# Row kurtosis on one core: load shapes, mixed sums, a halved last square, per-partition scaling and a warm TensorE

## The chip, the cores and the metric

The kernel runs on one core of one Trainium2 chip. The metric is device time in microseconds (us) of one execution, median over runs. All runs told here are of the state "fast". PE is TensorE, DVE is VectorE, ACT is ScalarE, POOL is GpSimd, SP is the engine that issues the loads. PSUM is the memory that this kernel has PE write its sums to (the pools `psum` and `psfin`).

## The reference

```python
# x: 1024 x 8192, float32
mean = np.mean(x, axis=-1, keepdims=True)
std = np.std(x, axis=-1, keepdims=True)
z = (x - mean) / (std + 1e-8)
return (np.mean(z ** 4, axis=-1) - 3).astype(np.float32)
```

With d = x - mean, the result per row is N sum(d^4) / (sum(d^2))^2 - 3. Every element is read once (33.5 MB), squared once after the mean is known, and squared again.

## The kernel before

The rows are worked in 18 groups; the results of several groups, a batch (`BATCHES`), are finished together and leave in one output transfer. A group of `k = 2` holds 64 rows, each split over two partitions, so a tile is 128 x 4096 float32 (2 MB). Group by group: PE transposes the tile in 128-column pieces and adds them up in PSUM, DVE adds partition pairs (`red`), a product gives the negated mean, ACT squares with the mean as bias and writes the sum of squares, then ACT does the first 512 columns of the fourth powers and DVE the other 3584.

```python
GROUPS = [(8, [1024], 0), (8, [1024], 0), (4, [2048], 0),
    (2, [2048, 2048], 512),            # ... ten of these, groups 3 to 12
    (2, [1536, 1536, 1024], 512),      # ... four, groups 13 to 16
    (2, [1536, 1280, 768, 512], 2816)] # group 17: k, pieces of the load, ACT's columns
BATCHES = [[0, 1], [2], [3, ..., 14], [15, 16, 17]]   # (cut)
# ...
small = ctx.enter_context(tc.tile_pool(name="small", bufs=4))
fin = ctx.enter_context(tc.tile_pool(name="fin", bufs=3))
# ... in finish(b), once for each batch:
kr = fin.tile([n, r], f32, name="kr")
nc.vector.tensor_mul(kr, p4, rec2)
nc.vector.tensor_scalar_add(kr, kr, -3.0)
dst = out[ROWS[b[0]]:ROWS[b[-1] + 1]].rearrange("(g r) -> g r", r=r)
nc.sync.dma_start(out=dst, in_=kr)
# ... the main part starts with all loads, on the same queue:
for i in range(NG):
    load(i)
```

Two things in these lines matter later. The pool `fin` gives each named tile `bufs` buffers in turn: with 2, the third `kr` takes the buffer of the first and waits until the transfer that reads the first is done (1.39 us of idle time in the changed kernel's trace, 3.71 in that of a_half); with 3 the fourth takes it, and in the traces of before and a_fin3 that one did not have to wait. And the four output transfers are issued by SP in program order, behind all the loads.

Of the kernel before, what the change touches and what calls it, by code (L numbers as in the profile page):

```python
# [7 lines left out]
f32 = mybir.dt.float32  # L8
bf16 = mybir.dt.bfloat16
AO = mybir.AluOpType  # L10
AF = mybir.ActivationFunctionType
P = 128
# [4 lines left out]
    (8, [1024], 0),  # L17
    (8, [1024], 0),
    (4, [2048], 0),
    (2, [2048, 2048], 512),  # L20
    (2, [2048, 2048], 512),
    (2, [2048, 2048], 512),
    (2, [2048, 2048], 512),
    (2, [2048, 2048], 512),
    (2, [2048, 2048], 512),
    (2, [2048, 2048], 512),
    (2, [2048, 2048], 512),
# [1 line left out]
    (2, [2048, 2048], 512),  # L29
    (2, [1536, 1536, 1024], 512),  # L30
    (2, [1536, 1536, 1024], 512),
    (2, [1536, 1536, 1024], 512),
    (2, [1536, 1536, 1024], 512),
    (2, [1536, 1280, 768, 512], 2816),
]
BATCHES = [[0, 1], [2], [3, 4, 5, 6, 7, 8, 9, 10, 11, 12, 13, 14], [15, 16, 17]]
SLOT_W = 4096
SLOTS = 12


@with_exitstack
def kernel(
    ctx: ExitStack,
    tc: tile.TileContext,
    x: bass.AP,
    out: bass.AP,
):
    nc = tc.nc
    n_rows, n_cols = x.shape
    neg_inv_n = -1.0 / float(n_cols)  # L50
    AX = mybir.AxisListType.X
    NG = len(GROUPS)
    L = NG - 1
    KS = [g[0] for g in GROUPS]
    ROWS = [sum(P // k for k in KS[:i]) for i in range(NG + 1)]
    assert ROWS[-1] == n_rows

    xpool = ctx.enter_context(tc.tile_pool(name="xpool", bufs=SLOTS))
    const = ctx.enter_context(tc.tile_pool(name="const", bufs=1))
    small = ctx.enter_context(tc.tile_pool(name="small", bufs=4))  # L60
    fin = ctx.enter_context(tc.tile_pool(name="fin", bufs=3))
    psum = ctx.enter_context(tc.tile_pool(name="psum", bufs=2, space=bass.MemoryType.PSUM))
    psfin = ctx.enter_context(tc.tile_pool(name="psfin", bufs=1, space=bass.MemoryType.PSUM))
    ctx.enter_context(tc.manual_schedule())

    warm = const.tile([P, 1], f32, name="warm")
    nc.vector.memset(warm, 0.0)
    nc.scalar.activation(out=warm, in_=warm, func=AF.Square)  # L68


    blk = {}

    def block_matrix(k):
        r = P // k
        b = const.tile([P, P], f32, name=f"blk{k}")
        v = b.rearrange("p (r k) -> p r k", k=k)
        nc.gpsimd.memset(b, neg_inv_n)
        nc.gpsimd.affine_select(  # L78
            out=v, in_=v, pattern=[[-k, r], [0, k]], base=0,
            channel_multiplier=1, compare_op=AO.is_ge, fill=0.0)  # L80
        nc.gpsimd.affine_select(  # L81
            out=v, in_=v, pattern=[[k, r], [0, k]], base=k - 1,
            channel_multiplier=-1, compare_op=AO.is_ge, fill=0.0)
        blk[k] = b

    for k in dict.fromkeys(k for k in KS if k > 2):
        block_matrix(k)
    ident = const.tile([P, P], f32, name="ident")
    nc.gpsimd.memset(ident, 1.0)
    nc.gpsimd.affine_select(  # L90
        out=ident, in_=ident, pattern=[[-1, P]], base=0,
        channel_multiplier=1, compare_op=AO.is_equal, fill=0.0)
    negcol = const.tile([P, 1], f32, name="negcol")
    nc.gpsimd.memset(negcol, neg_inv_n)
    block_matrix(2)
    junk = const.tile([P, 1024], bf16, name="junk")

    where = {}
    for b in BATCHES:
        n = len(b)  # L100
        sa = const.tile([P, 2 * n], f32, name=f"sa{b[0]}")
        sd = const.tile([P, n], f32, name=f"sd{b[0]}")
        nc.gpsimd.memset(sa, 0.0)
        for j, i in enumerate(b):
            where[i] = (j, n, sa, sd)

    xts = {}
    sums = {}
    nmus = {}

    def load(i):
        k, pieces, _ = GROUPS[i]
        w = n_cols // k
        assert sum(pieces) == w
        xt = xpool.tile([P, SLOT_W], f32, name="xt")
        xts[i] = xt[:, :w]
        src = x[ROWS[i]:ROWS[i + 1], :].rearrange("r (k w) -> (r k) w", k=k)
        c = 0
        for w in pieces:
            nc.sync.dma_start(out=xt[:, c:c + w], in_=src[:, c:c + w])  # L120
            c += w



    def row_sums(i):
        k = KS[i]
        xt = xts[i]
        w = n_cols // k
        if k == 2:
            tps = psum.tile([P, P], f32, name="tps")  # L130
            for c in range(0, w, P):
                nc.tensor.matmul(tps, lhsT=xt[:, c:c + P], rhs=ident,  # L132
                                 start=c == 0, stop=c == w - P, is_transpose=True)
            red = small.tile([P, P], f32, name="red")
            nc.vector.tensor_reduce(  # L135
                out=red.rearrange("p (r k) -> p r k", k=k),
                in_=tps.rearrange("p (r k) -> p r k", k=k).unsqueeze(2).to_broadcast(
                    [P, P // k, k, k]),
                op=AO.add, axis=AX)
            sums[i] = (red, negcol)  # L140
        else:
            part = small.tile([P, 1], f32, name="part")
            nc.vector.tensor_tensor_reduce(  # L143
                out=junk[:, :w // 2], in0=xt[:, :w // 2], in1=xt[:, w // 2:], scale=1.0, scalar=0.0,
                op0=AO.add, op1=AO.add, accum_out=part)
            sums[i] = (blk[k], part)

    def mean(i):
        mps = psum.tile([P, 1], f32, name="mps")
        lhs, rhs = sums[i]  # L150
        nc.tensor.matmul(mps, lhsT=lhs, rhs=rhs, start=True, stop=True)  # L151
        nmu = small.tile([P, 1], f32, name="nmu")
        nc.scalar.copy(nmu, mps)  # L153
        nmus[i] = nmu

    def square(i):
        j, n, sa, sd = where[i]
        nc.scalar.activation(out=xts[i], in_=xts[i], func=AF.Square, bias=nmus[i],  # L158
                             accum_out=sa[:, j:j + 1])

    def fourth_act(i):
        j, n, sa, sd = where[i]
        c = GROUPS[i][2]
        if c > 0:
            nc.scalar.activation(out=xts[i][:, :c], in_=xts[i][:, :c], func=AF.Square,  # L165
                                 accum_out=sa[:, n + j:n + j + 1])

    def fourth_dve(i):
        j, n, sa, sd = where[i]
        t = xts[i][:, GROUPS[i][2]:]  # L170
        nc.vector.tensor_tensor_reduce(  # L171
            out=t, in0=t, in1=t, scale=1.0, scalar=0.0,
            op0=AO.mult, op1=AO.add, accum_out=sd[:, j:j + 1])


    def finish(b):
        j, n, sa, sd = where[b[0]]
        k = KS[b[0]]
        r = P // k
        sel = blk[k].rearrange("p (r k) -> p r k", k=k)[:, :, 0]  # L180
        p2 = psfin.tile([n, r], f32, name="p2")
        nc.tensor.matmul(p2, lhsT=sa[:, 0:n], rhs=sel, start=True, stop=True)  # L182
        rec = fin.tile([n, r], f32, name="rec")
        nc.vector.reciprocal(rec, p2)  # L184
        yield
        rec2 = fin.tile([n, r], f32, name="rec2")
        nc.vector.scalar_tensor_tensor(
            out=rec2, in0=rec, scalar=-1.0, in1=rec, op0=AO.mult, op1=AO.mult)
        yield
        p4 = psfin.tile([n, r], f32, name="p4")  # L190
        nc.tensor.matmul(p4, lhsT=sa[:, n:2 * n], rhs=sel, start=True, stop=False)  # L191
        nc.tensor.matmul(p4, lhsT=sd, rhs=sel, start=False, stop=True)  # L192
        kr = fin.tile([n, r], f32, name="kr")
        nc.vector.tensor_mul(kr, p4, rec2)  # L194
        nc.vector.tensor_scalar_add(kr, kr, -3.0)  # L195
        dst = out[ROWS[b[0]]:ROWS[b[-1] + 1]].rearrange("(g r) -> g r", r=r)
        nc.sync.dma_start(out=dst, in_=kr)

    for i in range(NG):
        load(i)  # L200
    waiting = []
    for i in range(NG):
        row_sums(i)
        mean(i)
        square(i)
        if waiting and i < L:
            next(waiting[0], None)
        if i >= 1:
            fourth_dve(i - 1)
            for b in BATCHES:  # L210
                if b[-1] == i - 1 and i < L:
                    waiting.append(finish(b))
        if i < L:
            fourth_act(i)
        if waiting and i < L and next(waiting[0], "done") == "done":
            waiting.pop(0)
    for f in waiting:
        list(f)
    tail = [finish(b) for b in BATCHES if b[-1] >= L - 1]
    for f in tail:  # L220
        next(f)
        next(f)
    fourth_act(L)
    fourth_dve(L)
    for f in tail:
        list(f)


# [28 lines left out]
```

## Time and profile before

| | before |
|---|---|
| time | 98.63 us (98.38 to 98.84; the three runs known at the prediction; with the fourth the median is 98.73) |
| last load landed | 84.58 us |
| square of group 16 starts | 81.84 us |
| last square starts | 86.80 us |
| last result ready | 94.38 us |

The profiled span is 96.6 us; times within it count from its start. The landing is the last of the 16 marks that the trace has for a load, one for each transfer engine. The order to read in is: does the stream of loads end near the end of the span (no, 10 us before the last result), and what is the chain behind it. The lines are in the prediction.

### The profile page before, as it was taken

The page shows a single profiled execution, that of the slowest core. Times are in us where ns is not written, and L with a number is a line of the kernel's source. Part 1 is how long each engine was busy: PE and PEld are TensorE (multiplying, and loading weights), DVE is VectorE, ACT ScalarE, POOL GpSimd, SP SyncE. Part 2 cuts the span into 40 slices and gives each one's busy share as a digit, 9 for nine tenths or more (in the row PEclk, how much of TensorE's full clock was granted, in tenths as well). Part 3 has the DMA queues.
Part 4 walks back from the last instruction along what each step waited for, and adds up shares of the span by engine and source line. Part 5 has one row for each costly group of instructions (what it writes and reads, how often), then busy time and mean ns, then how long its engine had stood idle before and what let it go on. Part 6 is the DMA issues. An engine that isn't in the chain of part 4 may idle for free.

```text
span 96.6 us, 1451 instructions
## 1 busy us (share of the span) xinstructions
PE 67.5 (70%) x540; PEld 61.4 (64%) x540; DVE 72.2 (75%) x74; ACT 77.9 (81%) x86; POOL 4.7 (5%) x20
## 2 busy tenths in 40 slices
PE   0040699797959597979797979797978797950120
PEld 0040699696949496969686868696967696940010
DVE  0238600653969998989898989798989698999470
ACT  6055540299979889999999999899999899989960
POOL 6830000000000000000000000000000000000000
PEclk9999999999999999999999999999999999998555
DMA  1999999999999999999999999999999999200000
GB/s 47 398 395 410 420 427 427 434 431 424 414 410 424 434 417 417 417 431 427 400 431 417 431 404 420 395 427 407 423 409 421 407 419 395 113 1 0 0 0 0
DMA packets 5658, 33.64 MB, mean 348 GB/s; under 512 B 660, under 2 KB 660, under 8 KB 2964
## 3 DMA queue, kind: packets, MB, share of 16 engines
q1 hardware_dynamic: 5652, 33.56, 84.5%
q8 instruction: 4, 0.07, 0.3%
q14 instruction: 2, 0.02, 0.0%
HBM read 33.55 MB, written 0.00 MB: 347 GB/s over the span
## 4 chain that ended last, share of the span: by engine, by line
DMA 72%; PE 13%; ACT 7%; SPq 3%; DVE 2%; issue 1%; ACTq 0%
DMA xt<-in_x_dram 72%; PE tps L132 10%; ACT xt L158 4%; SPq L120 3%; ACT xt L165 3%; DVE red L135 1%; PE mps L151 1%; PE p L191 1%; PE p L192 0%; DVE kr L194 0%; PE p L182 0%; DVE kr L195 0%; ACTq L252 0%; ACTq L158 0%; ACT nmu L153 0%
## 5 line engine op out<-in xcount | busy, mean ns | idle before, releaser
L171 DVE CUSTOM_DVE_ANT_0 xt<-xt 128x3584 f32<-128x3584 f32 (+3 forms) x18 | 60.6, 3365 | 1.9 <-ACT nmu L153 1.1
L158 ACT ACTIVATE xt<-xt,nmu 128x4096 f32<-128x4096 f32 (+2 forms) x18 | 60.1, 3342 | 0.8
L132 PE MATMUL tps<-ident,xt 128*128 128x128 f32 x480 | 59.6, 283 | 1.0 <-DMA xt<-in_x_dram 1.0
L132 PEld LDWEIGHTS tps<-ident,xt 128*128 128x128 f32 x480 | 55.5, 148 | 3.1 <-DMA xt<-in_x_dram 2.6
L135 DVE TENSOR_REDUCE red<-tps 128x128 f32<-128x256 f32 x15 | 6.3, 423 | 11.7 <-PE tps L132 11.4
L153 ACT COPY nmu<-mps 128x1 f32<-128x1 f32 x18 | 2.7, 151 | 13.2 <-PE mps L151 13.2
L151 PEld LDWEIGHTS mps<-negcol,red 128*128 128x128 f32 x30 | 4.5, 188 | 13.1 <-ACT xt L158 6.5
L151 PE MATMUL mps<-negcol,red 128*128 128x1 f32 x30 | 5.4, 248 | 9.9 <-DVE red L135 7.0
L165 ACT ACTIVATE xt<-xt 128x512 f32<-128x512 f32 (+1 forms) x15 | 11.4, 759 | 0.5
L151 PE MATMUL mps<-part,blk 128*128 128x1 f32 x6 | 1.7, 353 | 9.0 <-DVE part L143 9.0
L151 PEld LDWEIGHTS mps<-part,blk 128*128 128x128 f32 x6 | 1.5, 312 | 9.2 <-POOL blk L78 5.2
L143 DVE CUSTOM_DVE_ANT_0 junk<-xt 128x512 bf16<-128x512 f32 (+1 forms) x3 | 2.7, 916 | 4.1 <-DMA xt<-in_x_dram 4.1
L182 PE MATMUL p<-blk,sa 128*2 128x16 f32 (+3 forms) x8 | 1.2, 232 | 4.2 <-ACT xt L158 4.2
L158 ACT ACTIVATION_READ_ACCUMULATOR xt<-xt,nmu 128x1 f32 x18 | 3.3, 185 | 0.0
L184 DVE RECIPROCAL rec<-p 2x16 f32<-2x16 f32 (+3 forms) x4 | 1.7, 418 | 2.1 <-PE p L182 2.1
L182 PEld LDWEIGHTS p<-blk,sa 128*2 128x2 f32 (+3 forms) x8 | 0.4, 84 | 4.3 <-issue 4.3
L165 ACT ACTIVATION_READ_ACCUMULATOR xt<-xt 128x1 f32 x15 | 2.8, 187 | 0.0
L191 PE MATMUL p<-blk,sa 128*2 128x16 f32 (+3 forms) x8 | 1.2, 233 | 2.2 <-ACT xt L165 2.2
L191 PEld LDWEIGHTS p<-blk,sa 128*2 128x2 f32 (+3 forms) x8 | 0.4, 84 | 2.5 <-ACT xt L165 2.5
L68 ACT ACT_TABLE_LOAD x1 | 1.3, 1283 | 0.8 <-PEq L241 0.8
L194 DVE TENSOR_TENSOR kr<-p,rec 2x16 f32<-2x16 f32 (+3 forms) x4 | 0.8, 189 | 1.4 <-PE p L192 1.4
L81 POOL TENSOR_SCALAR_AFFINE_SELECT blk<-blk 128x128 f32<-128x128 f32 x3 | 1.7, 564 | 0.2
(18 smaller groups left out, 8.7 us busy)
## 6 DMA issues: line engine op xcount, KB each, us to landing
xt<-in_x_dram SPq DMA_DIRECT2D x21, 1024.0 KB, 20.1
xt<-in_x_dram SPq DMA_DIRECT2D x9, 768.0 KB, 14.1
xt<-in_x_dram SPq DMA_DIRECT2D x6, 512.0 KB, 15.0
xt<-in_x_dram SPq DMA_DIRECT2D x1, 640.0 KB, 13.5
xt<-in_x_dram SPq DMA_DIRECT2D x1, 384.0 KB, 12.6
xt<-in_x_dram SPq DMA_DIRECT2D x1, 256.0 KB, 11.3
out_dram<-kr SPq DMA_DIRECT2D x2, 0.1 KB
out_dram<-kr SPq DMA_DIRECT2D x1, 3.0 KB
```

The source lines that it names most:

```text
L81: nc.gpsimd.affine_select(out=v, in_=v, pattern=[[k, r], [0, k]], base=k - 1, channel_multiplier=-1, compare_op=AO.is_ge, fill=0.0)
L120: nc.sync.dma_start(out=xt[:, c:c + w], in_=src[:, c:c + w])
L132: nc.tensor.matmul(tps, lhsT=xt[:, c:c + P], rhs=ident, start=c == 0, stop=c == w - P, is_transpose=True)
L135: nc.vector.tensor_reduce(out=red.rearrange("p (r k) -> p r k", k=k), in_=tps.rearrange("p (r k) -> p r k", k=k).unsqueeze(2).to_broadcast ...
L143: nc.vector.tensor_tensor_reduce(out=junk[:, :w // 2], in0=xt[:, :w // 2], in1=xt[:, w // 2:], scale=1.0, scalar=0.0, op0=AO.add, op1=AO.a ...
L151: nc.tensor.matmul(mps, lhsT=lhs, rhs=rhs, start=True, stop=True)
L153: nc.scalar.copy(nmu, mps)
L158: nc.scalar.activation(out=xts[i], in_=xts[i], func=AF.Square, bias=nmus[i], accum_out=sa[:, j:j + 1])
L165: nc.scalar.activation(out=xts[i][:, :c], in_=xts[i][:, :c], func=AF.Square, accum_out=sa[:, n + j:n + j + 1])
L171: nc.vector.tensor_tensor_reduce(out=t, in0=t, in1=t, scale=1.0, scalar=0.0, op0=AO.mult, op1=AO.add, accum_out=sd[:, j:j + 1])
L184: nc.vector.reciprocal(rec, p2)
L191: nc.tensor.matmul(p4, lhsT=sa[:, n:2 * n], rhs=sel, start=True, stop=False)
```

## The change

The intent: fewer and larger transfers early on; the last piece of groups 16 and 17 summed on DVE, so that fewer transposes follow the last landing; group 17 squared in two halves, so that DVE can start on the first; results scaled per partition with small instructions and regrouped batches; ten dummy products on PE, meant to bring it to full clock before group 3 (in the trace of before its transposes fell from 0.212 to 0.109 us each only at 16.9). The core of the diff:

```diff
-    (2, [2048, 2048], 512),      # groups 3 to 7
+    (2, [4096], 512),
-    (2, [1536, 1536, 1024], 512),
-    (2, [1536, 1536, 1024], 512),
-    (2, [1536, 1280, 768, 512], 2816),
+    (2, [1792, 1536, 768], 512),
+    (2, [1792, 1536, 768], 1024),
+    (2, [1536, 1280, 768, 512], 1408),
-BATCHES = [[0, 1], [2], [3, ..., 14], [15, 16, 17]]
+BATCHES = [[0, 1], [2], [3, ..., 12], [13, 14, 15, 16, 17]]
+MIXED = [16, 17]
...
-    fin = ctx.enter_context(tc.tile_pool(name="fin", bufs=3))
+    fin = ctx.enter_context(tc.tile_pool(name="fin", bufs=2))
...
+            tps = transposed_sums(i, c)          # mean(i), i in MIXED
+            part = added_halves(i, c)
+            nc.tensor.matmul(mps, lhsT=pair_sums(tps), rhs=negcol, start=True, stop=False)
+            nc.tensor.matmul(mps, lhsT=blk[k], rhs=part, start=False, stop=True)
...
+        kr = fin.tile([n, r], f32, name="kr")    # result(b, terms)
+        nc.vector.tensor_scalar_add(kr, pk, -3.0)
+        nc.sync.dma_start(out=dst, in_=kr)
...
+    STEPS = [(4, 5, 6), (7, 8, 9), (13, 14, 15)]  # groups at which a batch's three steps run
+    WARM = [3, 1, 4, 2]                           # dummy products ahead of groups 0 to 3
...
+    square(L, h, 2 * h)
+    fourth_dve(L - 1, GROUPS[L - 1][2])
+    square(L, 0, h, extra=1)
+    fourth_dve(L, h, 2 * h)
+    fourth_act(L, 0, a)
+    fac = factor(b)
+    ...
+    fourth_dve(L, a, h, extra=1)
```

(Cuts are marked; the comments and the shortened lists are mine. The smaller `fin` pool is part of the diff, though not of the intent above.)

More of the change, by code (lines that the diff above doesn't have):

```diff
@@ L19 @@
     (4, [2048], 0),
-    (2, [2048, 2048], 512),
-    (2, [2048, 2048], 512),
-    (2, [2048, 2048], 512),
-    (2, [2048, 2048], 512),
-    (2, [2048, 2048], 512),
+    (2, [4096], 512),
+    (2, [4096], 512),
+    (2, [4096], 512),
+    (2, [4096], 512),
+    (2, [4096], 512),
     (2, [2048, 2048], 512),
@@ L31 @@
     (2, [1536, 1536, 1024], 512),
-    (2, [1536, 1536, 1024], 512),
-    (2, [1536, 1536, 1024], 512),
-    (2, [1536, 1280, 768, 512], 2816),
+    (2, [1792, 1536, 768], 512),
+    (2, [1792, 1536, 768], 1024),
+    (2, [1536, 1280, 768, 512], 1408),
 ]
-BATCHES = [[0, 1], [2], [3, 4, 5, 6, 7, 8, 9, 10, 11, 12, 13, 14], [15, 16, 17]]
+BATCHES = [[0, 1], [2], [3, 4, 5, 6, 7, 8, 9, 10, 11, 12], [13, 14, 15, 16, 17]]
 SLOT_W = 4096
 SLOTS = 12
+MIXED = [16, 17]
+HALVES = 2
 @with_exitstack
@@ L64 @@
     ctx.enter_context(tc.manual_schedule())
-    warm = const.tile([P, 1], f32, name="warm")
-    nc.vector.memset(warm, 0.0)
-    nc.scalar.activation(out=warm, in_=warm, func=AF.Square)
+    zeros = const.tile([P, 256], f32, name="zeros")
+    nc.vector.memset(zeros, 0.0)
+    nc.scalar.activation(out=zeros[:, :1], in_=zeros[:, :1], func=AF.Square)
     blk = {}
@@ L98 @@
     where = {}
+    stats = []
     for b in BATCHES:
-        n = len(b)
-        sa = const.tile([P, 2 * n], f32, name=f"sa{b[0]}")
-        sd = const.tile([P, n], f32, name=f"sd{b[0]}")
-        nc.gpsimd.memset(sa, 0.0)
+        n = len(b) + (b[-1] == L)
+        s2, qa, qd = (const.tile([P, n], f32, name=f"{t}_{b[0]}") for t in ("s2", "qa", "qd"))
+        if any(GROUPS[i][2] == 0 for i in b):
+            nc.gpsimd.memset(qa, 0.0)
+        stats.append((s2, qa, qd))
         for j, i in enumerate(b):
-            where[i] = (j, n, sa, sd)
+            where[i] = (j, s2, qa, qd)
     xts = {}
-    sums = {}
     nmus = {}
@@ L121, in load @@
             c += w
-    def row_sums(i):
-        k = KS[i]
-        xt = xts[i]
-        w = n_cols // k
-        if k == 2:
-            tps = psum.tile([P, P], f32, name="tps")
-            for c in range(0, w, P):
-                nc.tensor.matmul(tps, lhsT=xt[:, c:c + P], rhs=ident,
-                                 start=c == 0, stop=c == w - P, is_transpose=True)
-            red = small.tile([P, P], f32, name="red")
-            nc.vector.tensor_reduce(
-                out=red.rearrange("p (r k) -> p r k", k=k),
-                in_=tps.rearrange("p (r k) -> p r k", k=k).unsqueeze(2).to_broadcast(
-                    [P, P // k, k, k]),
-                op=AO.add, axis=AX)
-            sums[i] = (red, negcol)
-        else:
-            part = small.tile([P, 1], f32, name="part")
-            nc.vector.tensor_tensor_reduce(
-                out=junk[:, :w // 2], in0=xt[:, :w // 2], in1=xt[:, w // 2:], scale=1.0, scalar=0.0,
-                op0=AO.add, op1=AO.add, accum_out=part)
-            sums[i] = (blk[k], part)
@@ L148, in mean, with transposed_sums, pair_sums @@
-    def mean(i):
-        mps = psum.tile([P, 1], f32, name="mps")
-        lhs, rhs = sums[i]
-        nc.tensor.matmul(mps, lhsT=lhs, rhs=rhs, start=True, stop=True)
+    def transposed_sums(i, w):
+        tps = psum.tile([P, P], f32, name="tps")
+        for c in range(0, w, P):
+            nc.tensor.matmul(tps, lhsT=xts[i][:, c:c + P], rhs=ident,
+                             start=c == 0, stop=c == w - P, is_transpose=True)
+        return tps
+    def pair_sums(tps):
+        red = small.tile([P, P], f32, name="red")
+        nc.vector.tensor_reduce(
+            out=red.rearrange("p (r k) -> p r k", k=2),
+            in_=tps.rearrange("p (r k) -> p r k", k=2).unsqueeze(2).to_broadcast(
+                [P, P // 2, 2, 2]),
+            op=AO.add, axis=AX)
+        return red
@@ new lines, in added_halves, with mean @@
+    def added_halves(i, c):
+        t = xts[i][:, c:]
+        h = t.shape[1] // 2
+        part = small.tile([P, 1], f32, name="part")
+        nc.vector.tensor_tensor_reduce(
+            out=junk[:, :h], in0=t[:, :h], in1=t[:, h:], scale=1.0, scalar=0.0,
+            op0=AO.add, op1=AO.add, accum_out=part)
+        return part
+    def mean(i):
+        k, pieces, _ = GROUPS[i]
+        mps = psum.tile([P, 1], f32, name="mps")
+        if k > 2:
+            nc.tensor.matmul(mps, lhsT=blk[k], rhs=added_halves(i, 0), start=True, stop=True)
+        elif i in MIXED:
+            c = sum(pieces[:-1])
+            tps = transposed_sums(i, c)
+            part = added_halves(i, c)
+            nc.tensor.matmul(mps, lhsT=pair_sums(tps), rhs=negcol, start=True, stop=False)
+            nc.tensor.matmul(mps, lhsT=blk[k], rhs=part, start=False, stop=True)
+        else:
+            tps = transposed_sums(i, n_cols // k)
+            nc.tensor.matmul(mps, lhsT=pair_sums(tps), rhs=negcol, start=True, stop=True)
@@ L154, in mean, with square @@
         nmus[i] = nmu
-    def square(i):
-        j, n, sa, sd = where[i]
-        nc.scalar.activation(out=xts[i], in_=xts[i], func=AF.Square, bias=nmus[i],
-                             accum_out=sa[:, j:j + 1])
-    def fourth_act(i):
-        j, n, sa, sd = where[i]
-        c = GROUPS[i][2]
-        if c > 0:
-            nc.scalar.activation(out=xts[i][:, :c], in_=xts[i][:, :c], func=AF.Square,
-                                 accum_out=sa[:, n + j:n + j + 1])
-    def fourth_dve(i):
-        j, n, sa, sd = where[i]
-        t = xts[i][:, GROUPS[i][2]:]
+    def square(i, c0=0, c1=None, extra=0):
+        j, s2, qa, qd = where[i]
+        t = xts[i][:, c0:c1]
+        nc.scalar.activation(out=t, in_=t, func=AF.Square, bias=nmus[i],
+                             accum_out=s2[:, j + extra:j + extra + 1])
@@ L171, in fourth_dve, with fourth_act @@
+    def fourth_act(i, c0, c1):
+        j, s2, qa, qd = where[i]
+        if c1 > c0:
+            t = xts[i][:, c0:c1]
+            nc.scalar.activation(out=t, in_=t, func=AF.Square, accum_out=qa[:, j:j + 1])
+    def fourth_dve(i, c0, c1=None, extra=0):
+        j, s2, qa, qd = where[i]
+        t = xts[i][:, c0:c1]
         nc.vector.tensor_tensor_reduce(
             out=t, in0=t, in1=t, scale=1.0, scalar=0.0,
-            op0=AO.mult, op1=AO.add, accum_out=sd[:, j:j + 1])
-    def finish(b):
-        j, n, sa, sd = where[b[0]]
+            op0=AO.mult, op1=AO.add, accum_out=qd[:, j + extra:j + extra + 1])
@@ new lines, in factor @@
+    def factor(b):
+        s2 = stats[BATCHES.index(b)][0]
+        n = len(b)
+        k = KS[b[0]]
+        p2 = psfin.tile([P, n], f32, name="p2")
+        if b[-1] == L:
+            nc.tensor.matmul(p2[:, :n - 1], lhsT=blk[k], rhs=s2[:, :n - 1], start=True, stop=True)
+            nc.tensor.matmul(p2[:, n - 1:n], lhsT=blk[k], rhs=s2[:, n - 1:n], start=True, stop=False)
+            nc.tensor.matmul(p2[:, n - 1:n], lhsT=blk[k], rhs=s2[:, n:n + 1], start=False, stop=True)
+        else:
+            nc.tensor.matmul(p2, lhsT=blk[k], rhs=s2, start=True, stop=True)
+        rec = fin.tile([P, n], f32, name="rec")
+        nc.vector.reciprocal(rec, p2)
+        fac = fin.tile([P, n], f32, name="fac")
+        nc.vector.scalar_tensor_tensor(
+            out=fac, in0=rec, scalar=-1.0, in1=rec, op0=AO.mult, op1=AO.mult)
+        return fac
@@ L178, in finish, with scaled, result @@
+    def scaled(b, fac, n):
+        s2, qa, qd = stats[BATCHES.index(b)]
+        w4 = fin.tile([P, len(b)], f32, name="w4")
+        nc.vector.tensor_add(w4[:, :n], qa[:, :n], qd[:, :n])
+        nc.vector.tensor_mul(w4[:, :n], w4[:, :n], fac[:, :n])
+        return w4
+    def result(b, terms):
+        n = len(b)
         k = KS[b[0]]
@@ L180, in finish @@
         sel = blk[k].rearrange("p (r k) -> p r k", k=k)[:, :, 0]
-        p2 = psfin.tile([n, r], f32, name="p2")
-        nc.tensor.matmul(p2, lhsT=sa[:, 0:n], rhs=sel, start=True, stop=True)
-        rec = fin.tile([n, r], f32, name="rec")
-        nc.vector.reciprocal(rec, p2)
-        yield
-        rec2 = fin.tile([n, r], f32, name="rec2")
-        nc.vector.scalar_tensor_tensor(
-            out=rec2, in0=rec, scalar=-1.0, in1=rec, op0=AO.mult, op1=AO.mult)
-        yield
-        p4 = psfin.tile([n, r], f32, name="p4")
@@ L191, in finish @@
-        nc.tensor.matmul(p4, lhsT=sa[:, n:2 * n], rhs=sel, start=True, stop=False)
-        nc.tensor.matmul(p4, lhsT=sd, rhs=sel, start=False, stop=True)
+        pk = psfin.tile([n, r], f32, name="pk")
+        for j, t in enumerate(terms):
+            nc.tensor.matmul(pk, lhsT=t, rhs=sel, start=j == 0, stop=j == len(terms) - 1)
         kr = fin.tile([n, r], f32, name="kr")
-        nc.vector.tensor_mul(kr, p4, rec2)
-        nc.vector.tensor_scalar_add(kr, kr, -3.0)
+        nc.vector.tensor_scalar_add(kr, pk, -3.0)
@@ L196, in finish, with warm_up @@
         dst = out[ROWS[b[0]]:ROWS[b[-1] + 1]].rearrange("(g r) -> g r", r=r)
         nc.sync.dma_start(out=dst, in_=kr)
+    def finish(b):
+        fac = factor(b)
+        yield
+        w4 = scaled(b, fac, len(b))
+        yield
+        result(b, [w4])
     for i in range(NG):
         load(i)
-    waiting = []
-    for i in range(NG):
-        row_sums(i)
+    STEPS = [(4, 5, 6), (7, 8, 9), (13, 14, 15)]
+    WARM = [3, 1, 4, 2]
+    warm = psfin.tile([P, 256], f32, name="warm")
+    def warm_up(n):
+        for _ in range(n):
+            nc.tensor.matmul(warm, lhsT=zeros[:, :P], rhs=zeros, start=True, stop=True)
@@ L204 @@
+    steps = {at: f for b, ats in zip(BATCHES[:-1], STEPS) for f in [finish(b)] for at in ats}
+    for i in range(L):
+        warm_up(WARM[i] if i < len(WARM) else 0)
         mean(i)
         square(i)
-        if waiting and i < L:
-            next(waiting[0], None)
         if i >= 1:
-            fourth_dve(i - 1)
-            for b in BATCHES:
-                if b[-1] == i - 1 and i < L:
-                    waiting.append(finish(b))
-        if i < L:
-            fourth_act(i)
-        if waiting and i < L and next(waiting[0], "done") == "done":
-            waiting.pop(0)
@@ L217 @@
-    for f in waiting:
-        list(f)
-    tail = [finish(b) for b in BATCHES if b[-1] >= L - 1]
-    for f in tail:
-        next(f)
-        next(f)
-    fourth_act(L)
-    fourth_dve(L)
-    for f in tail:
-        list(f)
+            fourth_dve(i - 1, GROUPS[i - 1][2])
+        if i in steps:
+            next(steps[i], None)
+        fourth_act(i, 0, GROUPS[i][2])
+    k, _, a = GROUPS[L]
+    h = n_cols // k // 2
+    b = BATCHES[-1]
+    n = len(b)
+    s2, qa, qd = stats[-1]
+    mean(L)
@@ new lines @@
+    square(L, h, 2 * h)
[3 more added lines that the diff above has]
+    fourth_act(L, 0, a)
+    fac = factor(b)
+    w4 = scaled(b, fac, n - 1)
+    wa = fin.tile([P, n], f32, name="wa")
+    nc.gpsimd.memset(wa, 0.0)
+    nc.scalar.activation(out=wa[:, n - 1:], in_=qa[:, n - 1:n], func=AF.Copy, scale=fac[:, n - 1:])
+    fourth_dve(L, a, h, extra=1)
+    nc.vector.scalar_tensor_tensor(
+        out=w4[:, n - 1:], in0=qd[:, n:], scalar=qd[:, n - 1:n], in1=fac[:, n - 1:],
+        op0=AO.add, op1=AO.mult)
@@ L230 @@
+    result(b, [wa, w4])
 _INS = ['x']
```

## The prediction

> **What bounds the kernel now.** I read the page first, for the engines' shares and the strip of slices, then the chain that ended last, then the timeline of both ends, and last the trace's DMA records.
>
> ```profile
> PE 67.5 (70%) x540; PEld 61.4 (64%) x540; DVE 72.2 (75%) x74; ACT 77.9 (81%) x86; POOL 4.7 (5%) x20
> ...
> ACT  6055540299979889999999999899999899989960
> ...
> PEclk9999999999999999999999999999999999998555
> DMA  1999999999999999999999999999999999200000
> ```
>
> The loads fill slices 2 to 34 of 40 at nine tenths or more: a stream of 33.5 MB, then about five slices (12 us) without loads. ACT is at eight or nine tenths in nearly every slice from the fifteenth to the thirty-eighth. So two limits run side by side, and only what shortens the stream or the tail behind it can move the end.
>
> ```profile
> 59.39 13.83 DMA xt<-in_x_dram
> 73.22 0.04 issue
> 73.27 2.42 PE tps L132 x20
> ...
> 78.31 2.42 PE tps L132 x20
> ...
> 81.94 3.66 PE tps L132 x32
> 85.60 0.02 issue
> 85.62 0.44 DVE red L135
> 86.06 0.14 issue
> 86.19 0.37 PE mps L151 x2
> ...
> 86.80 3.81 ACT xt L158 x2
> 90.61 0.02 issue
> 90.64 2.55 ACT xt L165
> ...
> 94.20 0.18 DVE kr L195
> ```
>
> This is the chain (start, length, what). Down to 73.22 it is transfers alone; then each late group runs landing, transposes, pair sums, mean, square. From the last square at 86.80 to the last result at 94.38 the chain takes 7.58 us, on ACT for most of it. The trace's landing marks (all 16 engines done) give group 14 at 69.46, group 15 at 74.50, 16 at 79.55 and 17 at 84.58: one group per 5.05 us. Squares 14 to 17 start 2.4, 2.4, 2.3 and 2.2 us after their landings. Between groups 6 (34.38) and 11 (57.62) ACT instead goes at its own pace of 4.65 us a group, quicker than the loads; from group 11 on it has caught up with them. Whatever is saved or lost before group 11 is therefore absorbed.
>
> ```profile
> 11.18 6.51 PE L132 MATMUL tps<-ident,xt 128*128 128x128 f32 x32 [0.28 <-DMA xt<-in_x_dram]
> ...
> 18.73 3.71 PE L132 MATMUL tps<-ident,xt 128*128 128x128 f32 x32
> ```
>
> The first 32 transposes took 6.51 us, the next 32 only 3.71: TensorE is slow at first. In the single records the step falls from 0.212 to 0.109 us at 16.9.
>
> [...] 0.212 against 0.109 us, and a grant of one half again from 88.6, three microseconds after the last burst. [...] 309 ns for 8 KB, 238 for 6, 159 for 4, 121 for 3, 84 for 2, so a fixed 9 ns or so. No packet of 16 KB on the load queue is in this trace. [...] The trace: 2002 ns at 2048 columns and 3723 at 4096, which is 0.840[...]. [...] the trace has 3883, and 2273 for 2048, 1491 for 1280.
>
> **The change part by part.** Whole-row loads, groups 3 to 7: two packets of 309 ns become one, by an estimate 9 + 2 x 300 = 609. That is 9 ns times 8 rows of an engine times 5 groups, 0.36 us less stream. The new cuts of 15 and 16 (7, 6 and 3 KB, an estimated 271 + 238 + 121 = 630 against 635) give 0.04 each. So landings 12 to 14 move 0.4 earlier, 15 to about 74.06, 16 to 79.07, 17 to 84.1. The cost: transposes of these groups can no longer begin on the first half. Group 3 lands near 13.5; warm, it takes 3.7 us and its square begins near 18.5 (was 18.86); cold it would begin near 21.5. Groups 4 to 7 are transposed at landing plus 3.7, within 0.5 us of now. All this lies before group 11, so neither the loss nor the warming shows at the end.
>
> Warm-up: ten products of 256 columns, [...] go into PE's gaps before 12 us. They can hold up the means of groups 1 and 2 by a few tenths. Worth nothing at the end, but needed so that whole rows do not hurt.
>
> Results per partition: reciprocals fall from 12x64 (541 ns) and 3x64 (546) to 10 and 5 columns. By the small cases (241 at 16, 346 at 32) this is about 0.2, so 0.35 us is saved in each batch. In the last batch the reciprocal lies under ACT's work.
>
> Now the last groups. Squares 12 and 13 start at 62.2 and 66.8, 14 at 71.5 (0.4 earlier, by ACT's pace). Group 15: last transpose 1.05 after landing, 75.1; pair sums, mean and copy take 1.22 as now (75.69 to 76.91), square at 76.35, now 76.91.
>
> Group 16, with its last 768 columns on VectorE: they are landed at 79.07, but VectorE does group 14's fourth powers (3.81 from start to start) from 75.55 to 79.36, then the result of the middle batch, 0.2. [...] the pair sums 0.42: 80.55. The mean is now two products of two passes, 0.65 for 0.35, and the copy 0.2: square at 81.48, now 81.84. Of the 0.36 all is the stream's; summing on VectorE saves transposes but waits for VectorE. ACT's share of group 16 doubles to 1024 columns: [...] 5.08 instead of 4.65. So ACT is free for the last square at 86.56.
>
> Group 17: group 15's fourth powers end at 84.39, the sum of 256 pairs 0.42, pair sums 0.42, mean and copy 0.85: ready at 86.1. ACT at 86.56 is later. The last square starts at 86.6, now 86.80: 0.2 gained.
>
> The tail, counted from 86.6. ACT: half square 2.12, half square 2.12, to 90.83; 1408 columns of fourth powers, [...] to 92.3; the scaled copy 0.25, to 92.6. VectorE: group 16 with 3072 columns from 85.3 for 3.28, to 88.6; the first squared half, 2048, 2.2, to 90.9; the sums of squares wait for ACT's 90.83 and a cold product 0.56 (as at 5.2 us now): 91.45; reciprocal 0.2, factor 0.2, add 0.17, multiply 0.17: 92.2; the last 640 columns 0.8: 93.0; scaling 0.2: 93.3; the product 0.35; minus three 0.2: 93.85. Now it is 94.38. So 0.2 before the square and 0.3 after: 0.5 us in all, and the output transfer behind it stays (94.4 to 96.6).
>
> 98.63 - 0.5 = 98.1; I put 98.0, since the estimates for small operations on the last stretch were rounded up.
>
> **The rivals.** First: VectorE becomes the bound of the tail. It has 3072, 2048 and 640 columns plus six small operations after 85.3 and no pause over 0.6 us; if the factor is later than I think, or an operation on one column costs 0.3, the end is at the old place: 98.5. For: VectorE is at eight or nine tenths in nearly every slice of the second half already. Against: its new small operations have few columns.
>
> Second: the late group is freed sooner than I say. If VectorE's wait before group 16 is not there, the square of 16 begins at 81.0 and all follows: 97.6. Against it stands that the fourth powers of 14 cannot start before the pair sums of 15 and take 3.88.
>
> Third: the stream gains more. Packets of 16 KB at the best rate seen in a slice (434 GB/s, so 604 ns) give 0.56 us instead of 0.36: 97.8. If the hardware cuts them in two, nothing: 98.4. The slowest of the 16 engines ends 2.0 us behind the first in the last loads; a shift of that lag, which grew by 0.9 where an instruction fetch of 16 KB crossed the stream at 26.75, moves the time by as much either way.
>
> Fourth: the Copy activation brings a table load on ACT at 92.3. It would end at 93.9 with the copy, later than VectorE: 98.7.
>
> Fifth: the intent succeeds in full, stage for stage, and the last landing alone sets the end: half a square (2 us) off the serial tail. It would be near 96.6. Against: VectorE's and ACT's columns in the tail are nearly the same in sum as now.
>
> **Range and chances.** The arithmetic gives 0.5 with terms unsure by 0.3 (tail), 0.3 (stream and lag) and 0.3 (start of the square); runs of before spread over 0.46. Together plus or minus 0.7 or so: 97.2 to 98.7. Faster by 2% means below 96.66, only in the fifth rival: 0.06. Slower by 2% (over 100.6) needs a new stall of 2 us, which nothing above gives: 0.02. Within 2%: 0.92.
>
> **What would show it.** Transposes of group 3 at 0.109 us and its square near 18.5; the last landing near 84.1; VectorE passing from fourth powers straight into the partial sum of 16; square 16 near 81.5 and the first half square near 86.6 with ACT, not TensorE, as what it came from; the chain's last part on VectorE instead of ACT; the last result near 93.85. It is wrong if the landing moves by more than 0.8 us, if ACT idles over 0.5 us before the last square, if a second table load shows, or if ACT's pace of 4.65 is still behind at group 12.

For terms of these sums the trace of before gives: on ACT the squares took 2002 ns at 2048 columns and 3723 at 4096, so 0.840 ns a column, which makes, as an estimate, 0.43 us for 512 columns more and 0.75 for 896 more, the latter on top of the 0.63 measured for 512. On DVE the fourth powers took 1491, 2273 and 3883 ns at 1280, 2048 and 3584 columns; the line through the first and the last gives, as an estimate, 0.56 us for 384 columns, 0.43 for 256 and 0.83 for 640. The one table load took 1283 ns; that the new Copy activation would bring no second one it could not show.

## The result, and the profile after

The changed kernel takes 103.27 us (102.58 to 103.54, 4 runs) where before takes 98.73 (98.38 to 99.75, 4 runs): ratio 1.043, 95% interval 1.034 to 1.053. It is slower. Ratios here are the mean time of one kernel's fast runs over that of the other's in the same rounds, so not quite the ratio of the medians.

The page's strip shows two things that before did not have: notches in PE's clock, and a DVE slice at six tenths, the thirty-third, shortly before the stream's end.

```profile
DVE  1255600375999179899998989898999968949970
...
PEclk9999976999995799999999999999999999587555
DMA  2999999999999999999999999999999981000000
```

The chain that ended last (start, length, what):

```profile
60.02 14.14 DMA xt<-in_x_dram
74.18 10.06 DMA xt<-in_x_dram
84.25 0.07 DVE part L149
84.32 0.35 DVE red L138
...
85.38 4.80 PE tps L132 x28
...
91.57 4.09 ACT xt L176 x4
...
98.50 0.21 DVE kr L228
```

From the last square to the last result it takes 98.71 - 91.57 = 7.14 us; I had forecast 7.25 (86.6 to 93.85). The tail is as forecast, it only starts 5 us late. The chain puts that down to a load, "74.18 10.06". But the landing mark of group 16 stands at 80.15, 3.6 us before DVE takes up that group's last piece (83.77): where the engine named has long been done, it was another. The timeline of DVE alone names it (in square brackets: idle time before, and its releaser):

```profile
78.34 3.89 DVE L188 CUSTOM_DVE_ANT_0 xt<-xt 128x3584 f32<-128x3584 f32 x1
82.16 0.08 DVE L188 DVE_READ_ACCUMULATOR2_ANT qd<- 128x1 f32 x1
83.63 0.21 DVE L228 TENSOR_SCALAR kr<-pk 10x64 f32<-10x64 f32 x1 [1.39 <-DMA out_dram<-kr]
83.77 0.54 DVE L149 CUSTOM_DVE_ANT_0 junk<-xt 128x384 bf16<-128x384 f32 x1
```

The third `kr`, an operation of 0.21 us, waits for an output transfer. With two buffers it takes over the buffer of the first `kr`, and the transfer of that one, though its data were ready at 40.3, was issued by SP only behind the last load:

```profile
74.18 0.33 SPq L126 DMA_DIRECT2D xt<-in_x_dram  x1
75.19 0.33 SPq L230 DMA_DIRECT2D out_dram<-kr  x1
```

It landed at 83.54, 8.35 us after its issue. The last output, with nothing ahead of it, was issued at 98.74 and landed at 99.88, in 1.1 us. What lay ahead of the first output on SP's queue the trace shows: at 75.19 seven loads were still to land, the last at 85.18, and the two packets of the little transfer, 64 bytes each, moved only at 82.37 and 82.92, in 11 ns each. That they stood behind the loads in flight is my reading of this; a_outq below tests it. (The output's landing, 83.54, comes before those of the last three of these loads: a load's landing is the mark of the slowest of the 16 engines, and the first engine was done with the last load at 82.66.)

Behind the wait stands a second loss. PE had finished group 16's transposes at 81.9 and waited for DVE. The windows view (busy time by engine, then PEclk) is cut here at the two ends of the half clock, 85.34 and 88.75, with as long a stretch before it:

```profile
81.93:85.34 3.41, 0.54 (x5) 0.57 (x6) 2.02 (x7) 1.75 (x4) 0.00 (x0) 1.00 0.33 129
85.34:88.75 3.41, 3.41 (x18) 3.41 (x18) 3.41 (x4) 3.30 (x2) 0.00 (x0) 0.50 0.00 0
```

PE was busy for 0.54 of 3.41 us, and in the next window its granted clock is 0.50. The 28 transposes of group 17 fall into it and take 4.92 us:

```profile
85.24 4.92 PE L132 MATMUL tps<-ident,xt 128*128 128x128 f32 x28
```

### The profile page after: what moved, and what is told of

Read it like the earlier page. It is cut to its first block, busy times and chain, and to the rows that moved or that the text cites. A ratio compares the mean times of both kernels' runs of the same rounds, so it can differ in the third digit from the quotient of the medians.

```text
span 100.8 us, 1467 instructions
## 1 busy us (share of the span) xinstructions
PE 74.5 (74%) x552; PEld 67.9 (67%) x552; DVE 73.9 (73%) x85; ACT 77.7 (77%) x89; POOL 5.1 (5%) x19
## 4 chain that ended last, share of the span: by engine, by line
DMA 78%; PE 7%; SPq 5%; ACT 4%; DVE 3%; issue 1%
DMA xt<-in_x_dram 78%; PE tps L132 5%; SPq L126 5%; ACT xt L176 4%; DVE xt L188 1%; DVE red L138 1%; PE mps L164 1%; PE p L202 1%; PE mps L165 0%; PE pk L226 0%; DVE w L278 0%; DVE kr L228 0%; DVE rec L206 0%; ACT nmu L170 0%; DVE fac L208 0%
## 5 line engine op out<-in xcount | busy, mean ns | idle before, releaser
L188 DVE CUSTOM_DVE_ANT_0 xt<-xt 128x3584 f32<-128x3584 f32 (+4 forms) x19 | 61.7, 3249 | 1.5 <-ACT xt L176 1.2
L132 PE MATMUL tps<-ident,xt 128*128 128x128 f32 x470 | 59.0, 288 | 3.3 <-DMA xt<-in_x_dram 3.3
L132 PEld LDWEIGHTS tps<-ident,xt 128*128 128x128 f32 x470 | 56.6, 151 | 4.0 <-issue 3.7
L183 ACT ACTIVATE xt<-xt 128x512 f32<-128x512 f32 (+2 forms) x15 | 10.6, 709 | 0.5
L247 PE MATMUL warm<-zeros 128*128 128x256 f32 x20 | 7.2, 504 | 2.3 <-ACT zeros L71 2.3
L149 DVE CUSTOM_DVE_ANT_0 junk<-xt 128x512 bf16<-128x512 f32 (+3 forms) x5 | 3.6, 728 | 4.7 <-DMA xt<-in_x_dram 4.7
L247 PEld LDWEIGHTS warm<-zeros 128*128 128x128 f32 x20 | 4.6, 248 | 2.9 <-ACT zeros L71 2.3
L81 POOL TENSOR_SCALAR_AFFINE_SELECT blk<-blk 128x128 f32<-128x128 f32 x3 | 2.2, 725 | 0.2
L201 PE MATMUL p<-s,blk 128*128 128x1 f32 x2 | 0.6, 363 | 2.1 <-ACT xt L176 2.1
L228 DVE TENSOR_SCALAR kr<-pk 2x16 f32<-2x16 f32 (+3 forms) x4 | 0.8, 189 | 1.9 <-DMA out_dram<-kr 1.4
```

The source lines that it names most:

```text
L132: nc.tensor.matmul(tps, lhsT=xts[i][:, c:c + P], rhs=ident, start=c == 0, stop=c == w - P, is_transpose=True)
L149: nc.vector.tensor_tensor_reduce(out=junk[:, :h], in0=t[:, :h], in1=t[:, h:], scale=1.0, scalar=0.0, op0=AO.add, op1=AO.add, accum_out=part)
L183: nc.scalar.activation(out=t, in_=t, func=AF.Square, accum_out=qa[:, j:j + 1])
L188: nc.vector.tensor_tensor_reduce(out=t, in0=t, in1=t, scale=1.0, scalar=0.0, op0=AO.mult, op1=AO.add, accum_out=qd[:, j + extra:j + extra ...
L247: nc.tensor.matmul(warm, lhsT=zeros[:, :P], rhs=zeros, start=True, stop=True)
```

## The experiments

All gave correct results. "Before" ran beside each; ratios are to it.

| label | edit | median us | ratio (95%) | third `kr` starts | last square | last result |
|---|---|---|---|---|---|---|
| changed kernel | | 103.27 | 1.043 (1.034, 1.053) | 83.63 | 91.57 | 98.71 |
| a_fin3 | 3 buffers | 98.18 | 0.995 (0.988, 1.001) | 79.34 | 86.37 | 93.52 |
| a_half | halves in 3 to 7 | 103.90 | 1.053 (1.046, 1.060) | 83.55 | 92.69 | 99.83 |
| a_fin3_half | both | 98.20 | 0.997 (0.990, 1.004) | 80.17 | 87.20 | 94.35 |
| b_whole | before, whole rows | 98.58 | 1.000 (0.994, 1.007) | | 87.72 | 95.29 |
| b_fin2 | before, 2 buffers | 98.79 | 1.003 (0.994, 1.011) | | 87.31 | 94.89 |
| a_late | third result one group later | 98.29 | 0.998 (0.991, 1.005) | 84.77 | 87.04 | 94.18 |
| a_outq | outputs from GpSimd | 98.38 | 1.000 (0.993, 1.008) | 79.92 | 86.96 | 94.10 |
| a_stallwarm | 5 products in the stall | 102.12 | 1.037 (1.029, 1.045) | 83.64 | 91.58 | 98.73 |
| a_stallwarm11 | 11 products in the stall | 102.00 | 1.035 (1.031, 1.039) | 83.61 | 91.37 | 98.52 |
| a_fin3_again | as a_fin3 | 98.18 | 0.996 (0.991, 1.000) | 79.51 | 86.55 | 93.70 |
| a_fin3_nowarm | 3 buffers, no warm-up | 98.29 | 0.998 (0.994, 1.002) | 79.61 | 86.64 | 93.79 |
| a_fin3_order | 3 buffers, DVE reordered | 97.81 | 0.992 (0.988, 0.996) | 80.06 | 87.09 | 93.94 |

Times of the last three columns are of the profiled execution, one for each kernel, in us from its start; "last square" is the start of group 17's square, of its first half where it is halved. The profiled execution need not be a typical one: a_fin3's took 97.37 us and that of its repetition 97.54, both near the fastest of their kernel (medians 98.18), b_whole's 99.11, its slowest.

### First set: the buffer, the loads, or the tail?

My theory (W) was the wait and the clock behind it. Rival R was the whole-row loads: in the changed kernel's trace group 6 was squared at 37.10 instead of 34.38, and ACT ran late from there on. Rival T was the new tail.

**a_fin3**

```diff
-    fin = ctx.enter_context(tc.tile_pool(name="fin", bufs=2))
+    fin = ctx.enter_context(tc.tile_pool(name="fin", bufs=3))
```

> The changed kernel with the buffers of the small result tiles put back from 2 to 3; nothing else. Theory W (the third result tile waits for the first result's output transfer, VectorE stands still from 82.2 to 83.6, and TensorE's clock drops behind it): the stall goes, group 16 is squared near 84.2 instead of 85.6, the last square starts near 89.3 instead of 91.6, and the time is about 101.0, because ACT is still some 2.5 us behind from the whole-row loads. Theory R (whole-row loads alone made the loss, the stall is hidden behind a late ACT): 103.0 or a little less. Theory T (halved squares and per-partition scaling made a worse tail): 103.0, tail of 7.1 us from the last square's start as before.

One digit gives 5 us back. Theory W holds and both rivals fall. It gave more than I had expected, and the same timeline of DVE shows why:

```profile
79.34 0.08 DVE L188 DVE_READ_ACCUMULATOR2_ANT qd<- 128x1 f32 x1
79.34 0.21 DVE L228 TENSOR_SCALAR kr<-pk 10x64 f32<-10x64 f32 x1
79.47 0.54 DVE L149 CUSTOM_DVE_ANT_0 junk<-xt 128x384 bf16<-128x384 f32 x1
```

Without the wait `kr` comes at 79.34, not at 82.2 as I had reckoned from the changed kernel's own trace. There ACT, and DVE behind it, happened to be 2.8 us late at group 15 (79.14 against 76.34 here), and this delay lay in front of a wait whose end is fixed. So the 1.39 us of idle time in that trace is not the wait's cost. The cost is the distance from 79.34 to 83.63: 4.3 us. A second execution with two buffers bears this out: in the trace of a_stallwarm (below) ACT was on time, group 15 squared at 76.35, and group 16 was still squared at 85.61, the very time of the changed kernel's trace. Nor do the whole rows make that lateness by themselves: a_fin3 has them too and squared group 6 at 34.16. In the changed kernel's trace group 6 landed at 30.43 instead of 29.15, and its transposes met a stretch of half clock (30.73 to 34.14), 5.35 us for 32.

**a_half**, the changed kernel with 2 buffers and the old loads:

```diff
-    (2, [4096], 512),            # groups 3 to 7
+    (2, [2048, 2048], 512),
```

> The changed kernel with groups 3 to 7 loaded in two halves again, 2 buffers for the results kept. Theory W: the wait ends when the output transfer lands, a moment that the loads set, not ACT's pace; VectorE comes to it earlier and waits longer (about 3 us), and the time stays 102.5 to 104. Theory R: ACT is no longer behind, the time falls to about 99 to 100.5.

The time stayed, as W said (103.90). DVE now reached the wait at 79.8 and stood longer, to the same moment:

```profile
83.55 0.21 DVE L228 TENSOR_SCALAR kr<-pk 10x64 f32<-10x64 f32 x1 [3.71 <-DMA out_dram<-kr]
```

**a_fin3_half**, both edits:

> Both put back: 3 buffers and halves. Theory W together with R (two causes, of which each hides the other): the prediction's own schedule comes true, last square near 86.9, last result near 94.1, time 98.4. If something third is at work (mixed sums on VectorE, halved squares), it stays above 99.5.

98.20, as expected, and the last result at 94.35 where I had expected 94.1. No third loss shows. What the whole rows are worth it does not settle: here the last load landed at 84.76, in a_fin3 at 83.95, but over all the traces the landing was 84.39 to 85.06 with halves (four traces) and 83.95 to 85.37 with whole rows (ten). The medians, 98.20 and 98.18, do not tell the two apart either.

**b_whole**, the kernel before with the five whole-row groups and nothing else:

> The kernel before with whole rows in groups 3 to 7 only, no warm-up. Theory R: TensorE starts 32 cold transposes only when the whole row is there, group 6 is squared near 37 instead of 34.4, and as ACT gains only 0.3 to 0.4 us a group on the loads it is still behind at the end: 100.0 to 100.8. If the lag is absorbed as the prediction said: 98.3.

98.58, so R as a loss in the median is out by itself too. Group 3 was squared at 21.02 instead of 18.86 and group 6 at 36.47 instead of 34.38; the last square came at 87.72 instead of 86.80. Of the two microseconds lost early in that trace, more than half was made up, and in the medians no loss is seen.

### Second set: what makes the wait

The refined theory (W2): two buffers hurt only because the third result is computed before the first result's transfer has landed.

**b_fin2**

```diff
-    fin = ctx.enter_context(tc.tile_pool(name="fin", bufs=3))   # in the kernel before
+    fin = ctx.enter_context(tc.tile_pool(name="fin", bufs=2))
```

> The kernel before with 2 buffers for the small result tiles instead of 3. Theory W2 (the buffer count hurts only where the third result is computed before the first result's transfer has landed): before computes its third result at 85.0, and the first transfer landed at 84.1, so nothing waits: 98.65, ratio within 1%. Rival (2 buffers cost by themselves): over 101.

Unchanged at 98.79: the same digit is harmless there. Its third result was computed at 85.54, after the first transfer had landed at 83.57. The changed kernel's regrouped batches brought the third result forward by 5 to 6 us (79.3 to 80.2 where nothing waits), and that is what met the smaller pool.

**a_late**

```diff
-    STEPS = [(4, 5, 6), (7, 8, 9), (13, 14, 15)]
+    STEPS = [(4, 5, 6), (7, 8, 9), (13, 14, 16)]
```

> The changed kernel with 2 buffers, the third result's last step moved from group 15 to group 16, so behind the fourth powers of group 15. W2: VectorE comes to it near 84.4, after the transfer's landing near 83.5, and does not wait: 98.2 to 98.7, as with 3 buffers. Rival as above: 103.

98.29, with two buffers. The third `kr` came at 84.77, the transfer had landed at 83.05, and DVE shows no wait for it:

```profile
84.77 0.21 DVE L228 TENSOR_SCALAR kr<-pk 10x64 f32<-10x64 f32 x1
```

**a_outq**

```diff
-        nc.sync.dma_start(out=dst, in_=kr)
+        (nc.sync if b[-1] == L else nc.gpsimd).dma_start(out=dst, in_=kr)
```

> The changed kernel with 2 buffers, the first three results' transfers issued from GpSimd instead of behind the loads on SP. W2: the first result, computed near 40, lands within a few us, the third finds its buffer free: 98.2 to 98.7. If instead the transfer were late because the 16 engines are full of loads whatever the queue: still near 103.

98.38, with two buffers and the early result. From GpSimd the first output is issued at 37.8 instead of 74 to 75. For the three transfers the view of the tile `kr` gives:

```profile
DMA to landing us min/median/max: 4.2/5.1/5.3
```

So among the loads a transfer of 128 bytes to 2.5 KB from another queue took 4.2 to 5.3 us; behind them on theirs the first output took 8.1 to 10.2 us in the other traces, on top of the late issue. Three cures that have nothing in common but the wait (one more buffer, a later step, another queue) give 98.2 to 98.4. This settles W2.

**a_stallwarm** leaves the wait in and fills PE's idle time behind it:

```diff
             part = added_halves(i, c)
+            if i == 16:
+                warm_up(5)
```

> The changed kernel with the wait left in, but five warm-up products put into TensorE's idle time between the transposes of group 16 and its mean. Theory C (TensorE's half clock after the stall costs about 0.9 us on top of it: 28 transposes in 4.9 us instead of 3.1): the last square starts 5.1 after square 16, by ACT's pace, instead of 6.0: 102.3. If the clock's drop costs nothing: 103.2.

The median, 102.12, fits, but the trace does not show what I meant it to. PE reached the products at 79.4, not 82, was done at 81.7, and the 28 transposes took 4.92 us as before. The number was too small for an execution in which ACT was not late; the run proves nothing.

**a_stallwarm11**, the same with `warm_up(11)`:

> As the run with five warm-up products in the stall, which in its profiled execution ended them at 81.7 and still lost the clock (28 transposes in 4.92 us): now eleven, some 5.1 us of work, so that TensorE is busy until the wait is over. Theory C: full clock for the transposes of group 17 (3.1 us), last square about 5.1 after square 16 instead of 6.0, last result 0.9 earlier: 101.7 to 102.3. If the clock is worth nothing here: 102.6 to 103.3, with the fast transposes to be seen all the same.

```profile
81.93:85.34 3.41, 3.41 (x17) 3.02 (x16) 1.74 (x5) 0.43 (x2) 0.00 (x0) 1.00 0.28 105
85.34:88.75 3.41, 3.41 (x32) 3.36 (x31) 3.41 (x4) 2.60 (x2) 0.00 (x0) 1.00 0.00 0
```

These are the same two windows as for the changed kernel: PE is busy throughout, and the clock stays whole. The transposes took 3.25 us instead of 4.92:

```profile
85.94 3.25 PE L132 MATMUL tps<-ident,xt 128*128 128x128 f32 x28
```

The last square came 5.06 us behind the square of group 16 (86.31 to 91.37) instead of 5.96 (85.61 to 91.57). That is the 0.9 us of theory C. The products ended at 85.74, though, and held up group 16's mean by 0.7, so the last result gained 0.2 only and not the 0.9 expected. The median, 102.00, lies in the forecast range, but its ratio's interval overlaps that of the changed kernel: the 0.9 us rests on the traces.

### Third set: what the rest of the change is worth

**a_fin3_again**

> The changed kernel with 3 buffers once more, with more rounds, as the measure for the next two: 98.2, ratio to before 0.995, as the prediction's sum says (0.5 us).

As expected: 0.996, interval up to 1.000. Without the wait the change is worth about half a percent, at the edge of what these runs can tell from nothing.

**a_fin3_nowarm**

```diff
-    WARM = [3, 1, 4, 2]
+    WARM = []
```

> 3 buffers, without the ten warm-up products. The prediction's account (lost time before group 11 is made up, since ACT gains on the loads): group 3 squared 1 to 2 us later, the end unchanged: 98.2, within 0.4. If whole rows need the warming: 99 or more.

98.29 against 98.18. Group 12 was squared at 62.41, in the repetition at 62.42, so no early difference is left by then. Not even at group 3 is there a steady gain: it was squared at 20.14 here, and at 18.12 to 21.59 in the eight traces with both whole rows and warm-up. In six of these PE's clock was not whole when group 3 landed (granted 0.50 from 13.66 to 17.07 in the changed kernel's) and its 32 transposes took 5.05 to 5.99 us, against 5.12 without warm-up; in two (a_fin3_again, a_stallwarm) they took 3.7 and the square came at 18.77 and 18.12.

**a_fin3_order** uses the tail's own numbers. In a_fin3 DVE stood idle for 0.33 us before the reciprocal, waiting for the sums of squares, with 640 columns of fourth powers still to do behind it.

```diff
+    fourth_dve(L, a, h, extra=1)
     fac = factor(b)
     w4 = scaled(b, fac, n - 1)
     ...
-    fourth_dve(L, a, h, extra=1)
```

> 3 buffers, and VectorE's last 640 columns of fourth powers put ahead of the factor, so that they fill its wait for the sums of squares (0.33 us) and the later steps: last result 0.3 to 0.4 us earlier than with 3 buffers alone: 97.8. If ACT's scaled copy sets the end instead: 98.1.

```profile
91.43 0.82 DVE L188 CUSTOM_DVE_ANT_0 xt<-xt 128x640 f32<-128x640 f32 x1
92.18 0.08 DVE L188 DVE_READ_ACCUMULATOR2_ANT qd<- 128x1 f32 x1
92.18 0.19 DVE L206 RECIPROCAL rec<-p 128x5 f32<-128x5 f32 x1
```

DVE goes from the fourth powers into the reciprocal without a gap; the tail from the last square is 93.94 - 87.09 = 6.85 us instead of 93.52 - 86.37 = 7.15 (93.70 - 86.55 = 7.15 in the repetition). The time is 97.81, ratio 0.992 (0.988 to 0.996): 0.8% below before, inside the 2% that count as the same, but clear of 1. That the new order itself is worth 0.3 us the traces show; the medians (97.81 and 98.18) agree, with intervals that overlap.

## Why the prediction was wrong

The forecast was 98.0 (97.2 to 98.7); measured were 103.27.

**The step that failed** stands in the working of group 16: "then the result of the middle batch, 0.2." The operation did take 0.21 us. What I had left out is when it may start: the line of the diff that takes the pool from 3 buffers to 2 is nowhere in my sum, and among the rivals none is about a buffer. Measured in its place: start at 83.63 instead of 79.34 (a_fin3), so 4.3 us, and then 0.9 for the transposes at half clock (5.96 against 5.06 us between the last two squares). Together they are the 5.2 us by which the last squares (91.57 and 86.37) and the last results (98.71 and 93.52) stand apart. Of the signs of being wrong that I had named, two show in the changed kernel's trace: ACT idle for over 0.5 us before the last square (0.79 us; before group 16's square 1.70), and ACT still behind at group 12, which was squared 5.2 us after its landing (65.21 and 60.01).

The trace of before held all that was needed. It shows output transfers issued only after the last load at 73.3, so from 74.5 on; my own schedule put the third result at 79.4; and the first output of before landed at 84.13, 9.6 us after its issue. Third result before first landing, two buffers: a wait. I read only the engines' instructions and the loads, and no output but the last.

**What held, once the wait was gone** (a_fin3, forecast in brackets): last load at 83.95 (84.1), square of group 16 at 81.31 (81.5), last square at 86.37 (86.6), last result at 93.52 (93.85); median time 98.18 (98.1 as the sum, 98.0 as put). The times within are those of an execution of 97.37 us, though, 0.8 below that median, so they are as good as forecast partly by luck. ACT was what the last square came from, by the doubled share of group 16: 5.06 us from square to square against 5.08. The fourth rival did not come: every one of the traces has a single table load, at the start (1283 ns in those of before and a_fin3).

**The 0.5 us and its terms.** From the last landing to the last result it was 9.80 and 9.83 us in the two traces of the old tail with ACT on time (before, b_fin2), and 9.52 to 9.62 in all six with the new tail, no wait and the old order of DVE. So behind the landing the change gains 0.2 to 0.3 us: 0.43 in the tail itself, less 0.2 because the last square starts 2.4 us after the landing instead of 2.2. The forecast had 9.75 for this stretch, so hardly any gain, and nearly all of its 0.5 in an earlier landing, which the traces do not show clear of their scatter. The size of the sum was right in part by luck. (Its terms for group 16 add up to 81.40, not 81.48; nothing hangs on that.)

**Whole rows.** The packets of 16 KB took 611 ns; I had estimated 609. Whether the stream's end moved by the 0.4 that I put on it is not shown. In a_fin3 and its repetition it looks so; over all ten traces with whole rows the last landing has a median of 84.47, over the four with halves 84.67, over ranges of 1.4 and 0.7 us. Much of that scatter is the lag that was among the rivals: in the last load the slowest engine was 1.6 to 2.8 us behind the first, 2.5 in the changed kernel's own trace (85.18).

**"Whatever is saved or lost before group 11 is therefore absorbed"** was right in substance (a_fin3_nowarm, b_whole in the medians), but it takes a whole stream: in the traces of the changed kernel and of b_whole ACT was still late at group 15. So too, "Worth nothing at the end, but needed so that whole rows do not hurt" was half right: warm-up is worth nothing that 98.29 against 98.18 could show, but whole rows did not need it either. And the sign that I had named for it, transposes of group 3 at 0.109 us each and the square near 18.5, failed in the changed kernel's trace: 5.07 us for the 32, which is 0.158 each in the mean, and 20.48. The warming had come early enough (PE's granted clock was 1.00 from 6.84 to 13.66), but the clock was 0.50 from 13.66 to 17.07, just when group 3 landed (14.08). The dummy products took 0.7 us each there (7.2 us for ten), and 0.7 and 0.9 in a_fin3 and its repetition.

**The fifth rival,** the intent in full, did not come: the tail from the last square to the last result fell from 7.58 to 7.15 us (a_fin3 and its repetition). The halved square, the scaling per partition and the new split of columns were not tried singly, nor were the sums on DVE, so their shares stay open.

## What to carry to other kernels

A buffer count is a wait that is written down nowhere: for each tile whose count falls, ask what last reads it, on which queue that reader stands and behind what, and compare that moment with the moment of the next use. If the reader is a transfer behind a stream of loads on the same queue, look for an end that is set by the stream and not by when its data were ready: here they were ready at 40.3, the transfer was issued at 75.19 and landed at 83.54. And do not take a wait's cost from the idle time in one trace: the changed kernel's showed 1.39 us, and the wait cost 4.3, because a delay of 2.8 us in front of it had vanished into a wait with a fixed end; the clock that fell behind it cost 0.9 on top.

## Further figures of these traces

- The clock: the stretches at half clock in the changed kernel's trace last 3.41 us each, but for the one at the end. The granted clock fell to 0.50 after a stretch of that length that held 1.75 us of PE work, its longest gap 1.06 us (window 27.32 to 30.73), as well as after stretches with 1.32 (longest gap 1.70) and 0.54 (2.87), and in the kernel before after one with 0.72 (85.22 to 88.63). Which share of work is enough no run here shows: in a_fin3_again the clock stayed whole after a window with 1.54 us of work (11.05 to 14.46).
- A small transfer: 8.35 us behind SP's loads in the changed kernel (8.1 to 10.2 over the traces), 4.2 to 5.3 from GpSimd's queue among them (a_outq), 1.1 with nothing ahead of it.
- Packets: those of the loads took (medians) 84 ns at 2 KB, 159 at 4, 309 to 312 at 8 and 611 at 16 KB, so the step from 8 to 16 KB gained 1 to 2%.
- Instruction fetches: one packet of 16 KB took 1.1 us at 28.3 in the changed kernel, and the lag between the first and the last of the 16 engines grew there from 1.0 to 2.7 us from one load to the next. That the one causes the other was not tried, and three later fetches of that size (44.9, 63.6, 77.8) left the lag in that trace at 2.6.
